# One DMA queue in the planner's order, by edges that order and do not wait

## The chip, the cores and the metric

The kernel runs on one core of one Trainium2 chip. A core has five engines with a queue of instructions each: TensorE (PE) for matmuls, VectorE (DVE), ScalarE (ACT) and GpSimd (POOL) for elementwise work, and SyncE (SP), which here issues every transfer between HBM and the core's memory. The metric is the device time of one launch in microseconds. Three runs of the kernel before took 2629.45 to 2636.64 us, median 2633.79.

## The reference

One layer of a hybrid trunk over 2048 positions of width 1024, in float32:

```python
h = rms_norm(x, norm_g)
z = h @ w_in
(aq, ak, av, af, az, bq, bk, bv, ba, bb, bz, mq, mz, gates) = _split_cols(z, IN_SIZES)
# three branches of h, each with a SiLU gate:
#   forgetting attention: 8 heads of 64, causal, score + cumsum(log_sigmoid(af + b_fg))
#   gated delta rule: 4 heads of 128, causal conv and SiLU ahead, state carried over chunks,
#     within a chunk a triangular solve with (A + I)
#   memory cross-attention: 4 heads of 128 against 256 rows of mem
# each branch @ w_branch, times sigmoid(gate + b_merge), summed; @ w_out; + x; final rms_norm
```

The comments stand for the functions of the reference. `af`, `ba`, `bb` are the few columns of logits (forget gates, decay and beta).

## The kernel before, in words

Every float32 product is made of three matmuls, of a high part and a low part of both operands. The input projection is cut into jobs. A job, `pd_in36` for instance, is one block of 128 columns of `w_in` against four groups of 512 positions, 24 matmuls each. Its weights come by `load_w`: `wr_in` (512 KB, two buffers) is loaded, ACT casts it to the high part `wh_in` (L381), POOL takes the difference as the low part `wl_in` (L385). The result of a group is emptied from PSUM into a tile `ev*`, of which there are three buffers, and stored from there (`evx` to `dv`, `evg` to `dgt`, `evl` to `dql`). Only when the store is done is the buffer free for the next group.

Beside the jobs run parts. `part_norm` makes h transposed. `part_logits` makes the logits: per group of 512 positions the matmuls `pslg`, a chain on ACT and DVE (`z`, `sg`, `e`, `l1`, up to the scan `loc` at L572), the store `dG` of the scan, and eight transposes `ptlg`. `part_gdn_inv` solves 32 x 32 blocks on DVE in two sets (`bk`, L903) and stores them as `dinv`. `part_gdn_b` reads `dinv` into `dd`, solves on from there (`pB` and later tiles), and carries the state from chunk to chunk (`chain`, with the loads `KQ`, `KV`, `Aq`, `zb`); the output of a chunk goes through `tail` (scaled, transposed in `pR`, multiplied by `zb`, stored to `dyb`). `part_fox` is the attention, with the loads `QA`, `QB`, `KA`, `KB`, `Vs`, `za`, `zl` per unit. At the end the branches are projected (`pbr`, `pba`, with the weights `wbr`, the gates `gt` and the partial sums `pp`) and the output projection `pout` follows.

What sets the order: a planner (`Plan`) keeps a clock per engine with costs of its own. Parts are generators, and each yields the time from which its next piece can run. The planner takes the pieces one after another, and so writes the program. A scheduler of the framework then gives every engine its queue out of the program: what is ready by the scheduler's own reckoning comes first, so that queue and program differ. An engine works its queue strictly in order. All transfers go through one function and so stand in SP's one queue, 1748 of them:

```python
    def move(dst, src, kb=0.0, after=0.0):
        nc.sync.dma_start(dst, src)
        return pl.dma(kb, after)
```

Its line 244 is the line of every SP row below.

Of the kernel before, what the change touches and what calls it, by code (L numbers as in the profile page):

```python
# [19 lines left out]
P = 128  # L20
EPS = 1e-6
INF = float("inf")
# [180 lines left out]
def later(*ws):  # L203
    return lambda: max(w() if callable(w) else w for w in ws)


def four(ps):
    return ps.rearrange("p (a b) -> p a b", a=4)
# [3 lines left out]
def tile_trunk(ctx, tc, x, mem, norm_g, w_in, w_v, w_lg, b_fg, b_mg, conv_w, a_log, dt_b,  # L212
               gdn_g, mem_g, w_kv, w_br, w_out, final_g, out):
    nc = tc.nc
# [7 lines left out]
    pl = Plan()  # L222
# [6 lines left out]
    def bc(ap, n):  # L229
        return ap.unsqueeze(2).to_broadcast([ap.shape[0], ap.shape[1], n])  # L230
# [12 lines left out]
# [3 lines that stand above are left out]
# [19 lines left out]
    dzb = [dram.tile([P, 4, 512], F32, name=f"dzb{g}") for g in range(NG)]  # L265
# [19 lines left out]
    def rsqrt(pool, dst, src, n, tag, after):  # L285

        yield after - AHEAD, 0.0
        s = pool.tile([P, n], F32, tag=tag + "s", name=tag + "s")
        nc.scalar.activation(s, src, AF.Sqrt)
        after = pl.op("act", 1.6, after)  # L290
        yield after - AHEAD, 0.0
        r = pool.tile([P, n], F32, tag=tag + "r", name=tag + "r")
        nc.vector.reciprocal(r, s)
        t = pool.tile([P, n], F32, tag=tag + "t", name=tag + "t")
        nc.vector.tensor_mul(t, r, r)
        nc.vector.tensor_mul(t, t, src)
        nc.vector.tensor_scalar(t, t, -0.5, 1.5, ALU.mult, ALU.add)
        nc.vector.tensor_mul(dst, r, t)
        return pl.op("dve", 0.9, after)
# [615 lines left out]
    def part_gdn_b():  # L915
# [7 lines left out]
        st = {"S": St0, "lev": 0, "chain": 0, "out": 0}  # L923

        def tmp(nm, tag, n):
            return gb.tile([P, 4, P], F32, tag=tag, name=nm, bufs=n)
# [63 lines left out]
        def chain():  # L990
            yield pl.pe + 2.0, 0.0
            for c in range(NCH):
                g, cc = divmod(c, 4)
                yield (lambda: 0.0 if st["out"] >= c - 1 else INF), 0.0
                KQ = gb.tile([P, 8, P], F32, tag="KQ", name="KQ")
                move(KQ, dkq[c], 512)
                KV = gb.tile([P, 8, P], F32, tag="KV2", name="KV2")
                move(KV, dkv[c], 512)
                Aq = tmp("Aq", "Aq", 1)
                td = move(Aq, dau[c][:, :, 1, :], 256)  # L1000
                zb = tmp("zb", "zb", 1)
                move(zb, dzb[g][:, :, cc * P:(cc + 1) * P], 256)
                St = st["S"]
                yield later(td, lambda: inv[c][1] - 1.5 if c in inv else INF, rc.when), 0.88
                E, te = inv[c]
                pZ, kb = rc.take("pZ")
                pZ = four(pZ)
                for h in range(4):
                    nc.tensor.matmul(pZ[:, h], KQ[:, h], St[:, h], start=True, stop=True)
                X = tmp("X", "ch", 3)  # L1010
                nc.vector.tensor_tensor(X, KV[:, 4:8], pZ, ALU.subtract)
                t1 = pl.dve(512, pl.pe + pl.LAT)
                rc.done(kb, t1)
                Se = tmp("Se", "ch", 3)
                nc.gpsimd.tensor_tensor(Se, St, bc(EGL[:, c, :], P), ALU.mult)
                ts = pl.pool(512, pl.pe)
                yield later(t1, te, rc.when), 0.88
                pY, kb = rc.take("pY")
                pY = four(pY)
                for h in range(4):  # L1020
                    nc.tensor.matmul(pY[:, h], E[:, h], X[:, h], start=True, stop=True)
                Y = tmp("Y", "ch", 3)
                nc.scalar.copy(Y, pY)
                t1 = pl.act(512, pl.pe + pl.LAT)
                rc.done(kb, t1)
                yield later(t1, rc.when), 0.88
                pS, kb = rc.take("pS")
                pS = four(pS)
                for h in range(4):
                    nc.tensor.matmul(pS[:, h], KV[:, h], Y[:, h], start=True, stop=True)  # L1030
                Sn = tmp("Sn", "St", 2)
                nc.vector.tensor_tensor(Sn, Se, pS, ALU.add)
                t2 = pl.dve(512, max(pl.pe + pl.LAT, ts))
                rc.done(kb, t2)
                yield later(t1, rg.when), 1.75
                pO, kb = rg.take("pO")
                pO = four(pO)
                for h in range(4):
                    nc.tensor.matmul(pO[:, h], KQ[:, 4 + h], St[:, h], start=True, stop=False)
                    nc.tensor.matmul(pO[:, h], Aq[:, h], Y[:, h], start=False, stop=True)  # L1040
                st["S"] = Sn
                st["chain"] = c + 1
                pl.add(tail(c, pO, kb, zb))

        def tail(c, pO, kb, zb):
            g, cc = divmod(c, 4)
            so = gb.tile([P, 4], F32, tag="so", name="so")
            jk = gb.tile([P, P], F32, tag="jk2", name="jk2")
            for h in range(4):
                nc.scalar.activation(jk, pO[:, h], AF.Square, accum_out=so[:, h:h + 1])  # L1050
            t1 = pl.op("act", 1.9, pl.pe + pl.LAT)
            yield t1 - AHEAD, 0.0
            nc.vector.scalar_tensor_tensor(so, so, 1.0 / P, WQ[:, c, :], ALU.mult, ALU.add)
            t1 = pl.op("dve", 0.3, t1)
            ro = gb.tile([P, 4], F32, tag="ro", name="ro")
            t1 = yield from rsqrt(gb, ro, so, 4, "gb", t1)
            ob = tmp("ob", "ob", 1)
            nc.vector.tensor_tensor(ob, pO, bc(ro, P), ALU.mult)
            t1 = pl.dve(512, t1)
            rg.done(kb, t1)  # L1060
            yield later(t1, rc.when), 0.44
            pR, kb = rc.take("pR")
            pR = four(pR)
            for h in range(4):
                nc.tensor.transpose(pR[:, h], ob[:, h], ident)
            nc.vector.scalar_tensor_tensor(zb, pR, gn_col, zb, ALU.mult, ALU.mult)
            e = pl.dve(512, pl.pe + pl.LAT)
            rc.done(kb, e)
            yield e - AHEAD, 0.0
            hi, lo = ob.bitcast(F32R), zb.bitcast(F32R)  # L1070
            nc.scalar.copy(hi, zb)
            e = pl.act(512, e)
            nc.gpsimd.tensor_sub(lo, zb, ob)
            e = pl.pool(512, e)
            yield e, 0.0
            for i, v in enumerate((ob, zb)):
                move(dyb[g][:, :, i, cc * P:(cc + 1) * P], v, 256, e)
            st["out"] = c + 1

        pl.add(chain())  # L1080
        pl.add(levels())
        yield (lambda: 0.0 if st["out"] == NCH else INF), 0.0
# [668 lines left out]
    pl.run(dense())  # L1751


def _layout(i):
    import numpy as np
    c = np.ascontiguousarray
    w = np.asarray(i["w_in"])[0]
    wd = np.concatenate([w[:, 0:1024], w[:, 1544:3592], w[:, 3600:]], axis=1)
    wl = np.concatenate([w[:, 1536:1544], w[:, 3592:3600]], axis=1)

    def chunks(m):
        k, n = m.shape
        return c(m.reshape(k // P, P, n // P, P).transpose(2, 1, 0, 3))

    wb = np.asarray(i["w_branch"])[0]
    return {
        "x": c(np.asarray(i["x"])[0]),
        "mem": c(np.asarray(i["mem"])[0]),
        "norm_g": c(np.asarray(i["norm_g"])[0]),
        "w_in": chunks(wd),  # L1770
        "w_v": c(w[:, 1024:1536].reshape(8, P, 512).transpose(1, 0, 2)),
        "w_lg": c(wl.reshape(8, P, 16).transpose(1, 0, 2)),
        "b_fg": c(np.asarray(i["b_fg"]).reshape(8, 1)),
        "b_mg": c(np.asarray(i["b_merge"]).reshape(24, P).T),
        "conv_w": c(np.asarray(i["conv_w"])[0].reshape(4, 12, P).transpose(2, 1, 0)),
        "a_log": c(np.asarray(i["a_log"]).reshape(4, 1)),
        "dt_b": c(np.asarray(i["dt_bias"]).reshape(4, 1)),
        "gdn_g": c(np.asarray(i["gdn_norm_g"]).reshape(P, 1)),
        "mem_g": c(np.asarray(i["mem_norm_g"])[0]),
        "w_kv": chunks(np.asarray(i["w_mem_kv"])[0]),  # L1780
        "w_br": c(np.stack([chunks(wb[n]) for n in range(3)])),
        "w_out": c(np.asarray(i["w_out"])[0].reshape(8, P, 1024)),
        "final_g": c(np.asarray(i["final_norm_g"])),
    }
# [17 lines left out]
```

## Time and profile before

| | |
|---|---|
| median of 3 runs | 2633.79 us |
| profiled execution | 2629.7 us, span 2627.6 us |
| PE busy | 2545.9 us, 97% |
| DVE, ACT, POOL busy | 1338.9, 1105.2, 1013.1 us |
| mean DMA rate | 149 GB/s |
| matmuls of the input projection (L401 to L403) | 3 x 1856, 0.39 to 0.40 us each |

The profiled execution is 2.1 us longer than its span, the part of a launch in which the profiled engines show nothing, and 4.1 us below the median. In a row of the profile the parts are: start in us, duration, engine, line, operation, the tile written and the tiles read, shapes, count, and in square brackets how long the engine had been idle before it and what ended that. A matmul of 512 columns shows 0.39 to 0.40 us, but the next one starts 0.23 us after it, since they are pipelined. SPq is SP's queue; an SP row is the issue of a transfer and not the transfer.

### The profile page before, as it was taken

The numbers are of one execution on the slowest core, as the hardware profiler recorded it, in microseconds if no ns is written. First come the engines' busy times: TensorE is split into PE (matmuls) and PEld (weight loads), VectorE is DVE, ScalarE is ACT, GpSimd is POOL, SyncE is SP. The second block draws the span as 40 slices with busy tenths as digits, with TensorE's granted clock in tenths as the row PEclk, the third lists the DMA queues.
The fourth block names the chain that finished last, engine by engine and source line by source line (L and its number), as shares of the span: only waits on it lengthen the run. The fifth ranks groups of instructions, "written<-read, shape, count | busy, mean of one in ns | idle before, by whom it ended". The sixth has DMA issues, their size and how long they took to land. (4 is left out here: it accounts for less than half of the span.)

```text
span 2627.6 us, 36711 instructions
## 1 busy us (share of the span) xinstructions
PE 2545.9 (97%) x12648; PEld 2112.2 (80%) x12648; DVE 1338.9 (51%) x2753; ACT 1105.2 (42%) x2287; POOL 1013.1 (39%) x818
## 2 busy tenths in 40 slices
PE   7998999999999999899999999999999999989998
PEld 6787888788888888688888888888887787877887
DVE  7452565656533337702222266666666677635433
ACT  5432234443475532134444446565556445323211
POOL 0101111221144334222232247777776768752110
PEclk9999999999999999999999999999999999999999
DMA  6223222222465564445555454344334768786432
GB/s 205 70 81 109 85 85 92 91 91 86 128 229 201 203 212 149 124 154 166 163 162 171 150 164 134 108 121 120 111 100 117 243 207 251 244 293 213 135 120 75
DMA packets 306050, 391.52 MB, mean 149 GB/s; under 512 B 62524, under 2 KB 185532, under 8 KB 305864
## 3 DMA queue, kind: packets, MB, share of 16 engines
q1 hardware_dynamic: 305864, 389.18, 46.5%
q8 instruction: 100, 1.64, 0.3%
q14 instruction: 86, 0.70, 0.1%
HBM read 238.78 MB, written 150.29 MB: 148 GB/s over the span
## 5 line engine op out<-in xcount | busy, mean ns | idle before, releaser
L401 PE MATMUL pd_in<-hh,wh_in 128*128 128x512 f32 x1856 | 746.6, 402 | 15.2 <-ACT evx L418 12.0
L403 PE MATMUL pd_in<-hh,wl_in 128*128 128x512 f32 x1856 | 728.2, 392 | 0.9
L402 PE MATMUL pd_in<-hl,wh_in 128*128 128x512 f32 x1856 | 726.0, 391 | 0.0
L385 POOL TENSOR_TENSOR wl_in<-wr_in,wh_in 128x1024 fp32r<-128x1024 f32 x84 | 202.5, 2411 | 626.0 <-ACT wh_in L381 597.8
L401 PEld LDWEIGHTS pd_in<-hh,wh_in 128*128 128x128 f32 x1856 | 350.1, 189 | 83.2 <-ACT evx L418 12.4
L403 PEld LDWEIGHTS pd_in<-hh,wl_in 128*128 128x128 f32 x1856 | 348.9, 188 | 78.6 <-POOL wl_in L385 4.0
L402 PEld LDWEIGHTS pd_in<-hl,wh_in 128*128 128x128 f32 x1856 | 350.3, 189 | 64.7
L1301 POOL TENSOR_TENSOR acc<-acc,ph 128x512 f32<-128x512 f32 (+3 forms) x288 | 318.9, 1107 | 55.7 <-ACT ph L1321 41.3
L1321 ACT ACTIVATE ph<-pst 128x512 fp32r<-128x512 f32 (+1 forms) x320 | 170.8, 534 | 159.7 <-PE pst L1315 81.2
L1278 DVE TENSOR_TENSOR plo<-pst,ph 128x512 fp32r<-128x512 f32 (+1 forms) x320 | 192.1, 607 | 83.3 <-ACT pst L1323 80.3
L1323 ACT ACTIVATE pst<-pst 128x512 f32<-128x512 f32 (+1 forms) x320 | 170.6, 533 | 0.0
L1573 POOL TENSOR_TENSOR gt<-gt,pp 128x512 f32<-128x512 f32 x64 | 86.7, 1358 | 191.6 <-DVE gt L1569 157.5
L381 ACT CAST wh_in<-wr_in 128x1024 fp32r<-128x1024 f32 x84 | 88.1, 1049 | 133.7 <-PE pd_in L402 119.2
L1188 DVE TENSOR_REDUCE nmx<-psm 128x1 f32<-128x512 f32 x192 | 128.5, 686 | 26.6 <-PE psm L1181 25.4
L1340 PE MATMUL po<-ph,Vs 128*128 128x512 f32 (+1 forms) x320 | 117.6, 368 | 1.1 <-ACT ph L1321 1.0
L474 DVE SCALAR_TENSOR_TENSOR evv<-xb,cw,evv 128x512 f32<-128x512 f32 x144 | 116.6, 810 | 3.7
L1314 PE MATMUL pst<-QA,KA 128*128 128x512 f32 (+1 forms) x320 | 116.2, 363 | 0.6 <-DVE QA L1196 0.6
L1315 PE MATMUL pst<-QB,KB 128*128 128x512 f32 (+1 forms) x320 | 116.6, 366 | 0.0
L1341 PE MATMUL pq<-plo,Vs 128*128 128x512 f32 (+1 forms) x320 | 116.1, 366 | 0.0
L1181 PE MATMUL psm<-KA,QA 68*128 68x512 f32 (+2 forms) x320 | 110.1, 375 | 4.6 <-DVE nmx L1188 3.0
L1541 PE MATMUL pbr<-yh,wbh 128*128 128x512 f32 x256 | 103.2, 404 | 9.3 <-DVE gt L1569 6.1
L1731 PE MATMUL pout<-woh,mh 128*128 128x512 f32 x256 | 100.1, 393 | 5.5 <-ACT woh L1643 5.5
(343 smaller groups left out, 4752.6 us busy)
## 6 DMA issues: line engine op xcount, KB each, us to landing
wr_in<-in_w_in SPq DMA_DIRECT2D x84, 512.0 KB
dgt<-evg SPq DMA_DIRECT2D x96, 256.0 KB
gt<-dgt SPq DMA_DIRECT2D x96, 256.0 KB
dpt<-gt SPq DMA_DIRECT2D x64, 256.0 KB
pp<-dpt SPq DMA_DIRECT2D x64, 256.0 KB
dgq<-evv SPq DMA_DIRECT2D x48, 256.0 KB
kqv<-dgq SPq DMA_DIRECT2D x16, 768.0 KB
xt<-in_x SPq DMA_DIRECT2D x16, 512.0 KB
```

Of the source, the lines that this page charges most:

```text
L385: nc.gpsimd.tensor_sub(lo, raw, hi.bitcast(F32))
L401: nc.tensor.matmul(ps, wh[:, k, :], xh[:, k, :], start=(k == 0), stop=False)
L402: nc.tensor.matmul(ps, wh[:, k, :], xl[:, k, :], start=False, stop=False)
L403: nc.tensor.matmul(ps, wl[:, k, :], xh[:, k, :], start=False, stop=(k == kt - 1))
L474: nc.vector.scalar_tensor_tensor(t, xb[:, j:j + 512], cw[:, wi, j:j + 1], t, ALU.mult, ALU.add)
L1188: nc.vector.tensor_reduce(mx, ps[:, 0:w], AX.X, ALU.max)
L1278: nc.vector.tensor_sub(plo[:, 0:w], ps[:, 0:w], ph[:, 0:w].bitcast(F32))
L1301: nc.gpsimd.tensor_add(acc[:, c0:512], acc[:, c0:512], ph[:, 0:w].bitcast(F32))
L1315: nc.tensor.matmul(ps[:, 0:w], KB[kt][:, ks], QBn[:, c0:512], start=False, stop=True)
L1321: nc.scalar.activation(ph[:, 0:w], ps[:, 0:w], AF.Exp, scale=0.125)
L1323: nc.scalar.activation(ps[:, 0:w], ps[:, 0:w], AF.Exp, scale=0.125)
L1340: nc.tensor.matmul(po[:, c0:512], V[:, 0:128], ph[:, 0:w], start=(t0 == 0), stop=(t0 == NT - 1))
```

## The change

It has two parts. At the end, when the planner has written the whole program, a loop goes through it and ties each transfer to the one before it on the same engine, by a dependency of the class NoSync. Such an edge binds the scheduler to the order and puts no semaphore wait into the queue. And the load of `zb` moves from `chain` into `tail`, which begins with a new condition: that the tail of the chunk before is through.

```diff
@@ -998,8 +998,6 @@
                 td = move(Aq, dau[c][:, :, 1, :], 256)
-                zb = tmp("zb", "zb", 1)
-                move(zb, dzb[g][:, :, cc * P:(cc + 1) * P], 256)
                 St = st["S"]
@@ -1040,10 +1038,13 @@
-                pl.add(tail(c, pO, kb, zb))
+                pl.add(tail(c, pO, kb))
 
-        def tail(c, pO, kb, zb):
+        def tail(c, pO, kb):
             g, cc = divmod(c, 4)
+            yield (lambda: 0.0 if st["out"] == c else INF), 0.0
+            zb = tmp("zb", "zb", 1)
+            move(zb, dzb[g][:, :, cc * P:(cc + 1) * P], 256)
@@ -1751,6 +1752,15 @@
     pl.run(dense())
 
+    last = {}
+    for i in list(nc.cur_bb.bb.instructions):
+        if isinstance(i, mybir.InstDMACopy):
+            if i.engine in last:
+                tc.add_manual_dep(i, last[i.engine].name, mybir.DependencyInfo(
+                    mybir.DependencyClass.NoSync, mybir.DependencyReason.DATA), reason="order")
+            last[i.engine] = i
```

The following rows show the queues that come out of it. The numbers at the tiles' names only tell them apart.

On SP near the start, before: the weights of job in36 stand among the first loads of `x`, ahead of everything that the logits store.

```order
L244 DMA xt_487<-in_x 128x1024
L244 DMA xt_491<-in_x 128x1024
L244 DMA wr_in36_0_1052<-in_w_in 128x1024
L244 DMA xt_627<-in_x 128x1024
L244 DMA xt_631<-in_x 128x1024
L244 DMA wr_in37_0_1113<-in_w_in 128x1024
```

The same loads in the changed kernel, some 25 transfers further on; `dG0` and `dG1` are the stores of the scan of the first two groups.

```order
L244 DMA dqh3_82<-evh_979 128x512
L244 DMA dql3_86<-evl_981 128x512
L244 DMA dG0_140<-loc_953 4x512
L244 DMA wr_in36_0_1052<-in_w_in 128x1024
L244 DMA dqh3_82<-evh_1048 128x512
L244 DMA dql3_86<-evl_1050 128x512
L244 DMA dG1_141<-loc_953 4x512
L244 DMA wr_in37_0_1113<-in_w_in 128x1024
```

The two weight loads have moved behind the scan's stores.

On PE at the same place, before: job in36 follows the last group of the first two jobs (`pdf1_3`).

```order
L403 MATMUL pdf1_3_983<-hh3_272,wl_in1_344 128x512
L401 MATMUL pd_in36_0_0_1109<-hh0_269,wh_in36_0_1056 128x512
L402 MATMUL pd_in36_0_0_1109<-hl0_273,wh_in36_0_1056 128x512
L403 MATMUL pd_in36_0_0_1109<-hh0_269,wl_in36_0_1058 128x512
L401 MATMUL pd_in36_0_0_1109<-hh0_269,wh_in36_0_1056 128x512
```

In the changed kernel the eight transposes `ptlg`, which read the scan, and the matmuls `pslg` of the second group (17 in all, of which the first two are shown) come between, and then job in36.

```order
L403 MATMUL pdf1_3_983<-hh3_272,wl_in1_344 128x512
L579 MATMUL ptlg_1060<-ident_63,loc_953 128x64
L580 MATMUL ptlg_1060<-ident_63,sg_1024 128x64
L579 MATMUL ptlg_1060<-ident_63,loc_953 128x64
L580 MATMUL ptlg_1060<-ident_63,sg_1024 128x64
L579 MATMUL ptlg_1060<-ident_63,loc_953 128x64
L580 MATMUL ptlg_1060<-ident_63,sg_1024 128x64
L579 MATMUL ptlg_1060<-ident_63,loc_953 128x64
L580 MATMUL ptlg_1060<-ident_63,sg_1024 128x64
L545 MATMUL pslg_1071<-hh1_270,wlh_932 128x512
L546 MATMUL pslg_1071<-hl1_274,wlh_932 64x512
```

Before, these transposes and matmuls stood in the middle of the job's third group; the next transposes, of the second group's scan, stand behind the job's fourth group in both kernels.

On SP while the inverse blocks are solved, before: the second set's `dinv1` stands between the stores of `dv2`.

```order
L244 DMA dv2_97<-evx_8835 128x4x128
L244 DMA dv2_97<-evx_8838 128x4x128
L244 DMA dinv1_195<-bk_8745 128x1024
L244 DMA dinv1_195<-tmp_8811 128x1024
L244 DMA dv2_97<-evx_8886 128x4x128
L244 DMA dv2_97<-evx_8889 128x4x128
L244 DMA dv3_98<-evx_8931 128x4x128
```

In the changed kernel it stands behind all of them, behind the gate stores `dgt` of the next jobs and ahead of the loads `U` and `dd` of the next stage.

```order
L244 DMA dv3_98<-evx_9054 128x4x128
L244 DMA dv3_98<-evx_9057 128x4x128
L244 DMA dgt0_115<-evg_9093 128x512
L244 DMA wr_in42_0_9135<-in_w_in 128x1024
L244 DMA dgt1_116<-evg_9129 128x512
L244 DMA dgt0_115<-evg_9163 128x512
L244 DMA wr_in43_0_9204<-in_w_in 128x1024
L244 DMA dgt1_116<-evg_9197 128x512
L244 DMA dinv1_195<-bk_8745 128x1024
L244 DMA dinv1_195<-tmp_8811 128x1024
L244 DMA dgt0_115<-evg_9230 128x512
L244 DMA U_9272<-dau0_160 128x4x128
```

The first set's `dinv0` moves likewise, from ahead of `dv1` to behind seven of its eight stores.

On SP where the attention begins, before: the load of a weight block for the second halves of the jobs, `wr_in42_2`, among the last chunks of the delta rule.

```order
L244 DMA Aq_12192<-dau15_175 128x4x128
L244 DMA dgt0_115<-evg_12202 128x512
L244 DMA wr_in42_2_12581<-in_w_in 128x1024
L244 DMA dgt1_116<-evg_12259 128x512
L244 DMA dyb3_126<-ob_12251 512x1x128
```

And in the changed kernel, behind the loads of the attention's first unit.

```order
L244 DMA KB0_12491<-dkh0_87 64x512
L244 DMA KB0_12491<-dkl0_91 64x512
L244 DMA Vs0_12506<-dv0_95 128x4x128
L244 DMA wr_in42_2_12581<-in_w_in 128x1024
L244 DMA dgt3_118<-evg_12473 128x512
```

It has moved past those unit loads and past the last stores of the delta rule. Elsewhere the weight loads move in the same way, from early places to the place that the planner gave them; the queues of PE, DVE, ACT and POOL hold the same work in nearly the same order (ACT has 10 fewer loads of an activation table, 102 for 112).

## The prediction

> **What bounds the kernel now.** I read the page's busy times and its costliest groups first, then the sync engine's waits, then the sequence of instructions around every place where TensorE stands still. From the page:
>
> ```profile
> PE 2545.9 (97%) x12648; PEld 2112.2 (80%) x12648; DVE 1338.9 (51%) x2753; ACT 1105.2 (42%) x2287; POOL 1013.1 (39%) x818
> L401 PE MATMUL pd_in<-hh,wh_in 128*128 128x512 f32 x1856 | 746.6, 402 | 15.2 <-ACT evx L418 12.0
> ```
>
> TensorE (PE) is busy 97% of the 2627.6 us span, in nearly the same order before and after the change. Only its idle time, about 80 us, and the slow restarts behind it can be won, and any new idle time is lost in full. The largest single wait is in the second row: 12.0 us on ACT's `evx`. The sync engine (SP) issues every transfer, and its waits by releaser say what held its queue up:
>
> ```profile
> SPq L244 <- POOL wl_in L385: 197.3, 65, 10.9
> SPq L244 <- DVE bk L903: 48.2, 2, 29.7
> SPq L244 <- DMA dyb<-zb: 29.2, 13, 3.8
> ```
>
> Columns are total us, times, longest. The middle row is two waits of `dinv` stores for the inverse chain on VectorE (DVE), one of 29.7 us. The timeline around it, SP, GpSimd (POOL) and PE:
>
> ```profile
> 1055.12 20.31 SPq L244 DMA_DIRECT2D dv<-evx  x14
> 1105.16 0.33 SPq L244 DMA_DIRECT2D dinv<-bk  x1
> 1106.66 9.66 SPq L244 DMA_DIRECT2D dv<-evx  x8
> 1076.37 2.11 POOL L420 TENSOR_TENSOR evx<-vf,evx 128x256 fp32r<-128x256 f32 x2 [1.33 <-ACT evx L418]
> 1102.77 0.39 PE L403 MATMUL pd_in<-hh,wl_in 128*128 128x512 f32 x1
> 1115.18 0.79 PE L401 MATMUL pd_in<-hh,wh_in 128*128 128x512 f32 x1 [12.03 <-ACT evx L418]
> 1122.77 0.39 PE L401 MATMUL pd_in<-hh,wh_in 128*128 128x512 f32 x1
> ```
>
> `evx` is finished at 1078.5, but its store goes out only at 1106.66, behind `dinv`; the three buffers stay full, ACT cannot empty PSUM, PE stands from 1102.77 to 1115.18. The group of 24 matmuls that follows takes 1122.77 - 1115.18 = 7.6 us.
>
> **The change part by part.**
>
> *Start, a cost.* In the new order the load `wr_in36` stands behind `dG0`, the store of the first scan `loc`, and PE's queue has the eight `ptlg` and the whole second `pslg` ahead of job in36 (both are in the rows above). Before:
>
> ```profile
> 13.37 0.38 SPq L244 DMA_DIRECT2D wr_in<-in_w_in  x1
> 87.20 0.59 ACT L551 COPY z<-pslg 64x512 f32<-64x512 f32 x1 [4.72 <-PE pslg L549]
> 88.39 0.39 PE L401 MATMUL pd_in<-hh,wh_in 128*128 128x512 f32 x1
> 88.41 1.05 ACT L381 CAST wh_in<-wr_in 128x1024 fp32r<-128x1024 f32 x1 [0.62 <-PE pdf L402]
> 89.54 2.40 POOL L385 TENSOR_TENSOR wl_in<-wr_in,wh_in 128x1024 fp32r<-128x1024 f32 x1 [6.58 <-ACT wh_in L381]
> 93.83 0.39 PE L401 MATMUL pd_in<-hh,wh_in 128*128 128x512 f32 x1
> 94.08 0.60 ACT L443 ACTIVATE evt<-pd_in 128x512 f32<-128x512 f32 x1
> 101.73 0.26 SPq L244 DMA_DIRECT2D dG<-loc  x1
> 121.38 0.24 PE L579 MATMUL ptlg<-ident,loc 64*128 64x64 f32 x1 [3.82 <-DVE loc L572]
> 121.99 0.51 PE L545 MATMUL pslg<-hh,wlh 128*128 128x512 f32 x1
> 127.36 0.39 PE L401 MATMUL pd_in<-hh,wh_in 128*128 128x512 f32 x1
> ```
>
> A weight load, from its issue to the cast that waits for it, alone and behind two others:
>
> ```profile
> 1008.13 0.33 SPq L244 DMA_DIRECT2D wr_in<-in_w_in  x1
> 1011.75 1.05 ACT L381 CAST wh_in<-wr_in 128x1024 fp32r<-128x1024 f32 x1 [2.36 <-DMA wr_in<-in_w_in]
> 1001.74 0.33 SPq L244 DMA_DIRECT2D wr_v<-in_w_v  x1
> 1008.35 1.05 ACT L854 CAST wvh<-wr_v 128x1024 fp32r<-128x1024 f32 x1 [2.22 <-DMA wr_v<-in_w_v]
> ```
>
> So 3.6 us alone, 6.6 in a crowd. The chain from `z` at 87.20 to `dG0` took 14.5 us; the cast (1.05) and the `evt` (0.60) of the job lie inside it on ACT and will not any more, so `dG0` goes at about 101.73 - 1.65 = 100.1, the load behind it at 100.4. It lands at 104.0, cast to 105.1, low part on POOL (2.40) to 107.5. PE stops at 88.39 until the scan is there, works off `ptlg` and `pslg` until about 105.5, and can go on with the job's third matmul at 107.5. A group of 24 takes 93.83 - 88.39 = 5.44 us, the job's four 21.8, of which two matmuls (0.45) are done: end at 128.9. Then `ptlg` of the next group, 0.6 us, without waiting: its scan starts from the `pslg` that ended by 105.5 and holds one `evt` of the first group (about 113), so it is there near 120, and the 3.82 us of today go. `pslg` begins at 129.5 and its 17 matmuls last 17 x 0.227 = 3.9 us, not the 127.36 - 121.99 = 5.4 of today, which came behind an idle stretch. Job in37 starts at 133.4 instead of 127.36: **+6.0 us**. Bounds: +4.5 (scan a further 1.5 us earlier) to +11 (landing 6.6, and the chain no shorter than today's 14.5). Jobs in37 to in39 keep 2 us or more by the same steps.
>
> The Trainium skill (TensorE: Matmul & The Clock Gate, "What's actually happening") says that the array's clock halves after an idle window of about 3.4 us and comes back after as much work. The trace agrees (the 3.82 us wait is followed by 1.5 us lost, the 12.03 us one by 2.2), and by that rule the 2 us before 107.5 cool nothing; with a landing of 6.6 they become 5 and some 1.7 us more, an estimate from that page, would be added.
>
> *Inverse chain, a gain.* `dinv0` moves behind seven `dv1` stores and `dinv1` behind the gate stores of job in41, so no `dv` store waits for DVE. The wait goes, 12.41 - 0.23 = 12.2, and the slow group after it, 7.59 - 5.44 = 2.15: **-14.3 us**. What could take its place is the first triangular solve, which reads `dinv`:
>
> ```profile
> 1119.12 4.60 SPq L244 DMA_DIRECT2D dd<-dinv  x8
> 1135.28 0.32 SPq L244 DMA_DIRECT2D dgt<-evg  x1
> 1156.77 0.49 PE L948 MATMUL pB<-dd,U 128*128 128x128 f32 x3
> ```
>
> All of PE comes 14.3 earlier here: the `dgt` store that now precedes `dinv1` goes at 1121, the eight `dd` loads take 4.6 us and one more gate store stands between, so they are out by about 1132 and `pB` is due at 1142.5. Ten us are left, so nothing is charged. The `dinv1` data themselves, 1105 today, are 4 us later, still ahead of 1121.
>
> *Weight loads in the middle.* They are no longer issued as soon as their buffer is free but behind the stores that the planner wrote first. The tightest are in3 and in20, of which this is in20, with the `dql` store that now stands ahead of its load:
>
> ```profile
> 253.09 0.32 SPq L244 DMA_DIRECT2D dql<-evl  x1
> 257.01 1.05 ACT L381 CAST wh_in<-wr_in 128x1024 fp32r<-128x1024 f32 x1 [4.67 <-PE pd_in L402]
> 260.59 0.50 PE L403 MATMUL pd_in<-hh,wl_in 128*128 128x512 f32 x1
> ```
>
> Issue at 253.4 and 3.6 us give 257.0, just the cast's time; with 6.6 PE loses 3.0. The others have their whole landing hidden by the 21.8 us of a job. I take 1 us for each of the two: **+2 us** (0 to +8, if six further jobs with a little more room lose 0.3 each).
>
> *First job of the attention stage.* `wr_in42_2` moves behind the key, query and value loads of unit 0, the last of which is the first row here; the second is the matmul that needs it.
>
> ```profile
> 1541.56 0.59 SPq L244 DMA_DIRECT2D Vs<-dv  x1
> 1546.48 0.40 PE L403 MATMUL pd_in<-hh,wl_in 128*128 128x512 f32 x1
> ```
>
> Issue 1542.2, landed 1545.8, cast 1546.8, low part 1549.3: **+3 us** (0 to +6, at 6.6).
>
> *Branch start, a gain.* Today `QA`, `QB` and `zl` loads stand ahead of `wbr`; now they follow it.
>
> ```profile
> 2026.38 0.38 SPq L244 DMA_DIRECT2D dgt<-evg  x1
> 2032.14 0.83 SPq L244 DMA_DIRECT2D wbr<-in_w_br  x2
> 2036.77 0.47 PE L1541 MATMUL pbr<-yh,wbh 128*128 128x512 f32 x1 [3.25 <-ACT wbh L1494]
> ```
>
> The 5.8 us from the store to `wbr` are the time in which those loads and the store pass the DMA engines; without the loads I take 2 off: **-2 us** (0 to -3.3, the whole wait of PE).
>
> *Second branch.* Its `gt` loads move later, each to its place beside the `pp` of its pair, in a stretch where the DMA engines are 84% busy and PE already waits for `gt`:
>
> ```profile
> 2255.00:2340.00 85.00, 78.91 (x347) 64.70 (x346) 37.43 (x52) 20.99 (x41) 58.59 (x48) 0.96 0.84 285
> 2333.36 0.80 PE L1541 MATMUL pbr<-yh,wbh 128*128 128x512 f32 x1 [5.00 <-DVE gt L1569]
> ```
>
> What was ahead of need becomes just in time: **+2 us** (-5, the whole wait, if the two loads of a pair arrive together; +6, as much again as the idle time of 85 - 78.91).
>
> *The `zb` load* goes into the output tail. It no longer holds SP for the store `dyb<-zb` (29.2 us in all), but nothing on PE waited for those; what it feeds is DVE's scaling behind the transpose `pR`. 0, at worst a us per stage if that cover is gone.
>
> **Sum:** +6.0 - 14.3 + 2 + 3 - 2 + 2 = -3.3. The profiled execution took 2629.7, the median is 4.1 above it; -3 from the median gives 2631 us.
>
> **The rivals.**
>
> *Late loads everywhere (slower).* My margins use today's ready times. If a store ahead of a load slips because its own buffer waits for a transfer, PE waits at each job start. The price is per job: 0.4 us in 60 jobs is 24 us, giving 2655. It decides from 11 us on, 0.2 us a job. For it speaks the 29.7 us row, a single store that stopped everything behind it; against it the 21.8 us that a job gives its successor's load of 7.1 (3.6 + 1.05 + 2.4). The Trainium skill (DMA: Bandwidth & Descriptors, "Anatomy of one DMA") states the rule under it, that a semaphore wait is served on the issuing sequencer before dispatch.
>
> *Gain without the bill (faster).* The crowding goes and the loads are all in time: 0 for the middle and the attention stage, +4.5 at the start, -5 in the second branch: -14.3 + 4.5 - 2 - 5 = -17, giving 2617. For it: SP's 197.3 us of waiting for `wl_in` are mostly loads asked for before their buffer was free, blocking stores behind them. Against: those waits stop no PE row but the one shown.
>
> *The inverse arrives late.* If `dd` lands after 1142.5, the won 12 us come back at `pB`: half of them gives 2638, all 2645. Against it the ten us above.
>
> **How the numbers follow.** The sum with its smaller uncertainties, 2623 to 2639: 0.40. Late loads everywhere, 2640 to 2665: 0.26. Gain without the bill, 2612 to 2623: 0.25. Late inverse: 0.09. A measurement of this kernel tells about 0.3%, 7.9 us, from no change, so same is 2625.9 to 2641.7. Faster: 0.25 and 0.06 from the low end of the first; slower: most of the second and 0.05 of the last, 0.30; the rest, 0.39, same. Leaving out a tenth on each side gives 2615 to 2654.
>
> **What would show it.** After: no PE wait on `evx` at 1103; `dv` stores without a stop; a new PE wait of some 11 us near 89 released by `loc`, a second of 2 at 105 by `wl_in`, none at 117; short `wl_in` waits at in20 and at 1546; `wbr` within 3 us of `dgt`. Wrong it is if `pd_in` shows waits on `wl_in` or `wh_in` at most jobs, or if `pB` waits for `dd`.

## The result, and the profile after

The changed kernel takes 2670.43 us (median of 4 runs, 2667.15 to 2674.16), the kernel before 2634.38 (4 runs, 2629.45 to 2636.64): a ratio of 1.014, 95% interval 1.012 to 1.016. It is 36 us slower, outside the predicted range. The profiled execution is the slowest of the four, 2674.16 us with a span of 2672.5; between the two profiles lie 44.9 us, and it is these that the traces below account for. They are more than the 36 us of the medians, since the profiled execution of the kernel before is 4 us faster than its median and this one 4 us slower.

From the page after, busy times and three groups; their columns are busy us, mean ns of one, and after the second bar the idle time ahead of them and what ended most of it:

```profile
PE 2561.9 (96%) x12648; PEld 2122.9 (79%) x12648; DVE 1317.6 (49%) x2753; ACT 1097.4 (41%) x2277; POOL 1020.7 (38%) x818
L401 PE MATMUL pd_in<-hh,wh_in 128*128 128x512 f32 x1856 | 749.6, 404 | 13.0 <-DVE evl L433 4.1
L403 PE MATMUL pd_in<-hh,wl_in 128*128 128x512 f32 x1856 | 730.0, 393 | 5.2 <-POOL wl_in L385 4.6
L381 ACT CAST wh_in<-wr_in 128x1024 fp32r<-128x1024 f32 x84 | 88.0, 1048 | 100.3 <-DMA wr_in<-in_w_in 74.0
```

The 12.0 us on `evx` are gone from the first group. The last row carries the loss. The page before has for the same group:

```profile
L381 ACT CAST wh_in<-wr_in 128x1024 fp32r<-128x1024 f32 x84 | 88.1, 1049 | 133.7 <-PE pd_in L402 119.2
```

Before, the cast of a weight block waited for a buffer that TensorE had to free: the data had long been there. Now ACT stands 74.0 us waiting for the load itself, while PE waits for `wl_in` only 4.6 us in all. Nearly half of the casts (40 of 84) wait for their load, and yet the projection's matmuls hardly do: besides those 4.6 us, PE waits once for `wh_in`, 3.6 us, and for the high and low parts of `w_v` 4.9 us. The stages show where the time goes. Busy us of PE, PEld, DVE, ACT, POOL with counts, the granted clock, the DMA share and GB/s, first before, then after:

```profile
0.00:240.00 240.00, 210.41 (x1030) 171.02 (x1031) 121.13 (x230) 105.13 (x163) 25.97 (x19) 0.97 0.35 116
440.00:600.00 160.00, 158.36 (x809) 129.33 (x808) 96.71 (x214) 76.04 (x187) 34.84 (x23) 1.00 0.29 97
760.00:1060.00 300.00, 296.81 (x1373) 245.02 (x1372) 134.72 (x289) 129.71 (x347) 116.01 (x100) 1.00 0.57 195
1060.00:1140.00 80.00, 67.97 (x287) 54.89 (x286) 44.11 (x62) 18.84 (x39) 24.45 (x26) 0.91 0.47 140
```

```profile
0.00:240.00 240.00, 194.98 (x930) 158.38 (x931) 118.37 (x226) 100.42 (x156) 20.83 (x17) 0.93 0.30 102
440.00:600.00 160.00, 151.02 (x788) 122.63 (x787) 100.90 (x227) 72.95 (x197) 29.86 (x19) 0.99 0.25 84
760.00:1060.00 300.00, 284.34 (x1301) 232.94 (x1300) 102.78 (x284) 146.41 (x387) 115.71 (x102) 0.97 0.61 204
1060.00:1140.00 80.00, 80.00 (x345) 64.44 (x344) 60.38 (x86) 16.64 (x43) 30.44 (x29) 1.00 0.39 112
```

PE loses busy time in the first three stages (the memory branch's attention is the second, the first stage of the delta rule the third) and is full in the fourth, where the inverse chain stood in its way before. In us, the lag of a kernel behind the one before at the same amount of TensorE work, from the start times of the matmuls in the profiled executions; the first column is the time at which the kernel before gets there, and the other kernels are those of the experiments:

| us before | after | weights free | gb free | weights, Gb free | stores only | stores from dv | dinv only |
|---|---|---|---|---|---|---|---|
| 80 | +2.7 | +1.9 | +2.2 | +3.2 | +0.9 | +0.3 | +1.7 |
| 160 | +11.5 | +2.7 | +10.9 | +2.9 | +1.7 | +1.0 | +1.6 |
| 204 | +19.4 | +7.7 | +18.5 | +7.7 | +6.8 | +1.1 | +1.5 |
| 440 | +22.3 | +7.6 | +21.6 | +7.9 | +6.8 | +0.8 | +2.6 |
| 600 | +31.5 | +7.6 | +29.4 | +8.1 | +7.2 | +0.8 | +2.6 |
| 1000 | +39.4 | +17.8 | +38.9 | +8.0 | +7.2 | +0.8 | +2.5 |
| 1040 | +51.9 | +22.1 | +47.6 | +10.6 | +7.2 | +0.8 | +2.5 |
| 1120 | +37.5 | +7.8 | +33.2 | -3.7 | -7.1 | -13.5 | -11.8 |
| 1520 | +37.1 | +7.7 | +32.8 | -3.8 | -7.2 | -13.6 | -11.9 |
| 1560 | +44.9 | +7.2 | +40.6 | -4.3 | -7.7 | -14.0 | -12.2 |
| 2000 | +43.0 | +4.1 | +39.2 | -7.5 | -5.7 | -11.5 | -11.3 |
| 2080 | +36.4 | +0.8 | +33.4 | -11.4 | -13.0 | -19.7 | -12.0 |
| 2160 | +43.1 | +5.5 | +40.4 | -8.0 | -12.1 | -19.0 | -11.9 |
| 2400 | +44.9 | +7.6 | +43.8 | -8.6 | -17.2 | -23.9 | -8.6 |

Each column is one execution against one. How far two executions differ on their own is seen in `zb_only` below, whose median is that of the kernel before: its lag is +0.4 to +0.6 from 80 to 2000, +1.9 at 2080 and 2160, and +5.0 at 2400. So steps of some 3 us behind 2000 say little.

In the places themselves: the start, where the load of job in36 stands behind the scan's store.

```profile
90.40 0.39 PE L401 MATMUL pdf<-hh,wh_in 128*128 128x512 f32 x1
102.08 0.27 SPq L244 DMA_DIRECT2D dG<-loc  x1
102.11 0.36 PE L579 MATMUL ptlg<-ident,loc 64*128 64x64 f32 x1 [10.85 <-DVE loc L572]
102.44 0.33 SPq L244 DMA_DIRECT2D wr_in<-in_w_in  x1
106.54 1.05 ACT L381 CAST wh_in<-wr_in 128x1024 fp32r<-128x1024 f32 x1 [9.58 <-DMA wr_in<-in_w_in]
107.67 2.37 POOL L385 TENSOR_TENSOR wl_in<-wr_in,wh_in 128x1024 fp32r<-128x1024 f32 x1 [90.46 <-ACT wh_in L381]
110.09 0.50 PE L403 MATMUL pd_in<-hh,wl_in 128*128 128x512 f32 x1 [0.89 <-POOL wl_in L385]
```

This is the predicted sequence, each step 2 to 2.6 us later than worked out; PE's stop at 90.40, before anything of it has happened, is 2.0 us late already. The inverse stage:

```profile
SPq L244 <- POOL evx L420: 68.2, 31, 5.0
1067.77 39.19 SPq L244 DMA_DIRECT2D dv<-evx  x15
1178.74 3.89 SPq L244 DMA_DIRECT2D dd<-dinv  x8
1194.29 1.05 PE L948 MATMUL pB<-dd,U 128*128 128x128 f32 x8
```

The `dv` stores wait for their own `evx`, at most 5.0 us (first row: total, times, longest), and between the two halves SP stands 4.7 us for `dinv` and `bk`, where one `dinv` held it for 29.7 before; PE is busy from 1060 to 1140, and the `dd` loads are out 11.7 us before `pB`, which waits for nothing. Two of the places that the prediction didn't charge: the `w_v` loads of the value jobs, and ahead of them the `Gb` load of a chunk.

```profile
1002.97 0.45 SPq L244 DMA_DIRECT2D Gb<-dG  x1
1009.41 0.21 ACT L789 ACTIVATE EGL<-Gb 128x4 f32<-128x4 f32 x1 [3.23 <-DMA Gb<-dG]
1013.02 1.30 POOL L829 TENSOR_TENSOR kqv<-kqv,eG 128x512 f32<-128x512 f32 x1
1014.35 0.32 SPq L244 DMA_DIRECT2D dkq<-kqv  x1
1039.50 0.43 SPq L244 DMA_DIRECT2D wr_v<-in_w_v  x1
1043.95 1.04 ACT L854 CAST wvh<-wr_v 128x1024 fp32r<-128x1024 f32 x1 [12.19 <-DMA wr_v<-in_w_v]
1045.05 0.52 PE L878 MATMUL pd_v<-wvh,hh 128*128 128x512 f32 x1 [3.03 <-ACT wvh L854]
1046.79 0.59 ACT L429 CAST evh<-pd_in 128x512 fp32r<-128x512 f32 x1 [1.79 <-DMA dkl<-evl]
1053.95 0.80 PE L401 MATMUL pd_in<-hh,wh_in 128*128 128x512 f32 x1 [2.69 <-DVE evl L433]
```

The store `dkq` waits in SP's queue until POOL is through with `kqv`, and every load behind it waits too. What comes late then stops ACT: 3.23 us for `EGL`, 12.19 us for `wvh`. PE waits 3.03 us for `wvh` and 1.91 for its low part. Behind `wvh` in ACT's queue stands `evh`, which empties the PSUM of the job before; DVE makes `evl` after it, and for that PE waits 2.69 us more. These are 7.6 of the 12.5 us between 1000 and 1040 in the table; in the rest the matmuls behind the waits come 0.43 us apart and not 0.23.

### The profile page after: what moved, and what is told of

Its sections match the earlier page's. It is cut to its first block, busy times and chain, and to the rows that moved or that the text cites. A ratio compares the mean times of both kernels' runs of the same rounds, so it can differ in the third digit from the quotient of the medians.

```text
span 2672.5 us, 36427 instructions
## 1 busy us (share of the span) xinstructions
PE 2561.9 (96%) x12648; PEld 2122.9 (79%) x12648; DVE 1317.6 (49%) x2753; ACT 1097.4 (41%) x2277; POOL 1020.7 (38%) x818
## 5 line engine op out<-in xcount | busy, mean ns | idle before, releaser
L453 ACT ACTIVATE evg<-pd_in,bmg 128x512 f32<-128x512 f32 x96 | 66.0, 687 | 123.3 <-PE pd_in L403 111.3
L474 DVE SCALAR_TENSOR_TENSOR evv<-xb,cw,evv 128x512 f32<-128x512 f32 x144 | 108.2, 751 | 3.6
```

## The experiments

Each time stands against runs of the kernel before on the same chip. Where only some transfers are tied, `move` takes a flag, and the loop ties each flagged transfer to the flagged one before it; lines are then some numbers lower down.

**Which transfers bring the loss.** First the `zb` move alone, with no edges.

```diff
-    last = {}
-    for i in list(nc.cur_bb.bb.instructions):
...
```

> The zb load in the tail, without the ordering edges. Theory of the late casts (the loss is that weight loads and a few other loads come late, so that the instruction that waits for them blocks its engine's queue): nothing to do with zb, the time of before within 4 us, 2630 to 2638. Theory that the zb move itself costs (SP waits, the tail's new condition): 2642 or more.

2634.09 us against 2633.55, ratio 1.0002 (0.9992 to 1.0013): nothing, so the loss comes with the edges. The edges with `zb` left where it was weren't tried. Next the planner's order for everything but the loads of weights (`w_in`, `w_kv`, `w_v`, `w_br`, `w_out`).

```diff
-            return raw, move(raw, src, kt * 64)
+            return raw, move(raw, src, kt * 64, tie=False)
...
```

> All transfers keep the planner's order except the loads of weights (w_in, w_kv, w_v, the branch and output weights), which the scheduler may hoist as before. Late casts: the steps of the changed kernel at the start (11.5 us), in20 (2), the memory branch's attention (9), the w_v loads (12.5) and in42 (8) go, the gain at the inverse chain (-14) stays, the memory rows' 9 and the delta rule's 6 stay: 2618 to 2636. Rival, the stores' strict order holds the output buffers: at most the start comes back, 2652 or more.

2634.01 us, 0.9998 (0.9988 to 1.0008). Without the order on the weight loads the whole loss of 36 us is gone; it is no gain yet, since the lag of 14.5 us from 600 to 1040 takes back what `dinv` brings. Its page:

```profile
L384 ACT CAST wh_in<-wr_in 128x1024 fp32r<-128x1024 f32 x84 | 88.2, 1050 | 136.1 <-PE pd_in L405 125.4
```

The cast waits for its load no more; for `Gb`, which is still tied, ACT's `EGL` waits 49.5 us in this run (9.8 in the kernel before). Then the opposite: all as before, except that the `dv` stores, the load of `bk` and the `dinv` stores are tied among themselves.

```diff
-                move(dinv[s][:, 0], E.rearrange("p j i -> p (j i)"), 512)
+                move(dinv[s][:, 0], E.rearrange("p j i -> p (j i)"), 512, tie=True)
...
```

> The kernel before, with edges only among the stores of dv, the load of bk and the stores of dinv; zb as before. Both theories: the 12 us wait on evx and its slow restart go and nothing else moves: 2617 to 2623, the wait at 1103 absent. If the gain needs the whole queue in order, 2630 or more.

2618.51 us, 0.9939 (0.9922 to 0.9956). The table shows the step between 1040 and 1120: -14.3.

**What else is late.** The weights and also `kqv` and `Gb` free:

```diff
-                nxt[c] = kqv, Gb, move(Gb, dG[g][:, cc * P:(cc + 1) * P].partition_broadcast(P), 256) + 1.0
+                nxt[c] = kqv, Gb, move(Gb, dG[g][:, cc * P:(cc + 1) * P].partition_broadcast(P), 256, tie=False) + 1.0
...
```

> As the one with free weights, and the loads of kqv and Gb (delta rule, first stage) free too. Late loads in general: the 6 us lost there come back besides, so 4 to 9 us less than with free weights alone, about 2612 to 2630. If only weights matter: the same as with free weights within 2 us.

2620.45 us, 0.995 (0.9935 to 0.9965): from 720 to 1040 the lag grows by 2.5 us and no longer by the 14 of the run before. With the loads of `x` and of the memory rows free as well:

```diff
-        return xt, move(xt, src[row: row + P, :], 512)
+        return xt, move(xt, src[row: row + P, :], 512, tie=False)
...
```

> The planner's order for all transfers except the loads of weights, kqv and Gb, and now also the loads of x and mem tiles and of the memory norm's scale. Late loads: the 2 to 3 us lost before 80 us and the 5 lost at the memory rows (near 204) come back too: 2609 to 2617. If these were lost to something else: 2619 to 2622, as with weights and Gb free.

2623.19 us against 2632.04, 0.9965 (0.995 to 0.998), a miss: the lag at 204 us is +6.0 and was +7.7. So the loss at the memory rows isn't their loads' place in the order alone. And `kqv` and `Gb` alone free, with the weights tied:

> The planner's order for all transfers but kqv and Gb; the weight loads stay late. The runs so far give the loads of the weights 2669 - 2634 = 35 us and, with those free, kqv and Gb another 13.5. If the two costs add (theory: each is a stop of ACT at its own place), the time is 2669 - 13.5, about 2656 (2651 to 2661), and the lead at 1000 us is some 8 us below that of the changed kernel while the 9 us at 440 to 560 and the 9 us at 180 to 206 stay. Rival: they hide one another (a load that waits anyway makes the other free), and 2664 to 2670 comes out, or they add up to more because a late Gb also makes weight loads late, below 2651.

2670.53 us against 2631.04, 1.0144 (1.0127 to 1.0161). The costs don't add. Between 600 and 1040 the lag grows by 20.4 us with both late, 18.2 with only the weights late, 14.5 with only `kqv` and `Gb` late, 2.5 with neither: the two late loads cost mostly the same time, and taking one away leaves the other. The rival that they hide one another holds, the time half a us above its 2664 to 2670.

**Stores alone.** The planner's order for the stores; every load free.

```diff
-            outs.ask(e, lambda: move(dh[g][:, i, :], th.bitcast(F32), 256))
+            outs.ask(e, lambda: move(dh[g][:, i, :], th.bitcast(F32), 256, tie=True))
...
```

> Edges among the stores alone, in the planner's order; every load is free. Late loads: nothing is lost any more, and the 14 us at the inverse chain are won: 2609 to 2618. Rival, the strict order of the stores holds output buffers and costs by itself: 2625 or more.

2616.17 us against 2632.04, 0.9936 (0.9918 to 0.9954): the gain at `dinv`, a further one at the branches, and a loss of 5.1 us between 160 and 204. To place that one, the same from the first `dv` store on only:

```diff
-        if tie:
+        if tie and n >= begin[0]:
...
```

> Stores alone in the planner's order as in stores_only, but only from the first dv store (about 1055 us) on; before it nothing is tied. It tells what the 7 us of lost time at 204 us of stores_only come from. Theory: from the edges between the stores of the start (dqh, dql, dG, dF), so that here the lead at 204 to 1040 us is that of dinv_only, +1.5 to +2.7, and the time is 2616 - 5 = 2611 (2607 to 2615). Rival: the loss at 204 comes from the order of the engines' queues that the scheduler makes anyway, or is won back later in stores_only; then 2614 to 2619.

2608.76 us against 2631.04, 0.9918 (0.9898 to 0.9937), the lowest ratio of all. It overlaps with that of `stores_only`, so that the 5 us rest on the lag: it is +1.1 at 204 and was +6.8, and what differs up to there is the order of the early stores. The wait of 12.0 us on `evx` is gone from the first group of its page:

```profile
L406 PE MATMUL pd_in<-hh,wh_in 128*128 128x512 f32 x1856 | 745.5, 402 | 3.2 <-DVE evt L449 3.0
```

**How a late load costs time where PE doesn't wait for it.** The memory branch's attention loses 9.2 us between 440 and 600. In the changed kernel at its second late block, job in35:

```profile
504.23 0.42 SPq L244 DMA_DIRECT2D wr_in<-in_w_in  x1
508.81 1.05 ACT L381 CAST wh_in<-wr_in 128x1024 fp32r<-128x1024 f32 x1 [1.33 <-DMA wr_in<-in_w_in]
509.93 2.39 POOL L385 TENSOR_TENSOR wl_in<-wr_in,wh_in 128x1024 fp32r<-128x1024 f32 x1 [8.14 <-ACT wh_in L381]
509.96 2.45 DVE L687 TENSOR_SCALAR mst<-mst 128x2 f32<-128x2 f32 x2
512.46 0.47 ACT L691 ACTIVATE pr<-psc,mst 128x256 f32<-128x256 f32 x1 [2.60 <-DVE mst L687]
514.21 0.63 PE L709 MATMUL ptm<-ident,pr 128*128 128x128 f32 x4 [2.25 <-DVE pr L697]
```

Two things meet the softmax: the cast stands in ACT's queue ahead of `pr`, and the subtraction, which follows the cast at once, runs on POOL just as DVE has its small step `mst` to do. PE waits 2.25 us for the softmax and not for a weight. In one run the cast and with it the subtraction of the three blocks in question were put 12 us later into the program:

```diff
+    LATE = ("in34_0", "in35_0", "in18_0")
-            return raw, move(raw, src, kt * 64)
+            return raw, move(raw, src, kt * 64) + (12.0 if nm in LATE else 0.0)
...
+            if nm in LATE:
+                tc.add_manual_dep(new, q[-2].name, ...)
```

> The changed kernel, in which only the casts of three weight blocks (in34, in35, in18) are placed 12 us later in ScalarE's queue, by the planner's time and an edge; their loads stand where they stood but for what follows from that. Theory that a late weight load hurts where its cast blocks ScalarE's queue: the 9 us lost between 440 and 570 fall to 0 to 3, in all 2660 to 2665, and the waits of the transposes ptm for the softmax there fall below 1 us. Rival, the weights or the DMA traffic reach TensorE late by themselves: no change, 2668 to 2673, or worse.

2667.02 us against 2632.04, 1.0132 (1.011 to 1.0153), 2 us above the expected range; the stretch loses 2.0 us, as expected, and no `ptm` waits longer than 0.5. To part the two, the subtraction alone later, the cast where it was:

```diff
+            if nm in LATE:
+                pl.at(t, lambda: cast(raw))
+                t += 12.0
...
```

> The changed kernel, in which for the three jobs in34, in35 and in18 only the subtraction on POOL (wl_in) is put 12 us later into the program and tied behind POOL's instruction before it, as in casts_later; the cast (wh_in) stays where the changed kernel has it in ACT's queue, ahead of the softmax's pr. It tells which of two stops the memory attention. Theory ACT: the late cast stops ACT and the pr behind it; then the stretch from 440 to 600 us loses what the changed kernel loses there, +7 to +9 us. Theory POOL: the subtraction, which follows the cast at once, falls on the softmax's small steps on DVE (mst, 2.38 us beside wl_in in the changed kernel, 0.16 without), and DVE waits for it; then the stretch loses +2 to +4, as casts_later does with +2.0, since the casts alone still cost some 0.8 us. Total 2664 to 2672 in both.

2670.46 us against 2633.79, 1.0139 (1.0121 to 1.0157), and the stretch loses 5.1 us, between the two expectations. At the same place:

```profile
500.26 1.05 ACT L389 CAST wh_in<-wr_in 128x1024 fp32r<-128x1024 f32 x1 [1.36 <-DMA wr_in<-in_w_in]
501.38 0.29 DVE L705 TENSOR_SCALAR mst<-mst 128x2 f32<-128x2 f32 x2
502.91 0.62 DVE L715 TENSOR_SCALAR pr<-pr,mst 128x256 f32<-128x256 f32 x2
503.41 0.63 PE L727 MATMUL ptm<-ident,pr 128*128 128x128 f32 x4
```

The cast still waits for its load, 1.36 us (1.33 in the changed kernel), and stands ahead of `pr`, but PE waits for nothing here. Across this block, from 484 to 488 us of the kernel before, the lag stays at 18.9, where in the changed kernel it grows from 27.4 to 29.7; at the other two blocks it doesn't grow either. The 5.1 us come in three steps of 1.5 to 1.7 further on, each where the moved subtraction now falls:

```profile
512.89 2.38 POOL L398 TENSOR_TENSOR wl_in<-wr_in,wh_in 128x1024 fp32r<-128x1024 f32 x1
514.32 1.37 DVE L715 TENSOR_SCALAR pr<-pr,mst 128x256 f32<-128x256 f32 x2
515.48 0.70 PE L727 MATMUL ptm<-ident,pr 128*128 128x128 f32 x4 [1.23 <-DVE pr L715]
```

The two `pr` of the next head take 1.37 us beside it and not 0.62, and PE waits 1.23. So it is the subtraction that costs, beside `mst` or beside `pr`, wherever it falls on a step of the softmax on DVE; the late cast ahead of `pr` costs nothing that the lag shows. With both moved, 2.0 us stay, in three steps of 0.7 to 0.9 whose cause is open. The times of these runs say nothing between them: 3 us are within their scatter, and the reading rests on one profiled execution of each.

Last, every cast tied behind the instruction that the program has ahead of it on ACT, so that no cast stands earlier in ACT's queue than the planner put it:

```diff
+                tc.add_manual_dep(new, q[-2].name, mybir.DependencyInfo(
+                    mybir.DependencyClass.NoSync, mybir.DependencyReason.DATA), reason="cast")
...
```

> The changed kernel, in which every cast of an input weight block keeps its place in the program behind the ScalarE instruction ahead of it, so that the scheduler cannot hoist it. Theory of the blocked queue: a part of the loss comes back, where the planner's place is later than the scheduler's, 2650 to 2666. Rival: unchanged, 2668 to 2673.

2684.75 us against 2632.04, 1.0196 (1.0176 to 1.0217), a miss. The memory attention no longer loses (43.2 to 43.9 us of lag from 440 to 600), but from 240 to 400 the lag grows from 24.3 to 43.3, and now it is the projection that waits; its PE waits:

```profile
PE pd_in L408 <- POOL wl_in L390: 12.8, 11, 1.3
PE pd_in L406 <- ACT wh_in L381: 10.6, 9, 3.0
```

With loads this late, the planner's place for all casts is no better: what the memory attention wins is lost where PE waits for the casts themselves.

## Why the prediction was wrong

**The step that failed** is the sentence "The others have their whole landing hidden by the 21.8 us of a job", with the bill of +2 us (0 to +8) under *Weight loads in the middle*. With the weight loads alone taken out of the order, the kernel is 36 us faster (2634.01 us for 2670.43). The margin was taken from the time at which PE needs the low part. But before PE a load meets ACT and POOL, whose queues the scheduler orders by its own reckoning: ACT waits 74.0 us for the loads, and the subtraction on POOL, the emptying of PSUM and the softmax of other parts shift with it or fall on one another. For in3 and in20, where PE is the one that waits, the term held: the lag grew by 0.8 at in3 and by 1.4 at in20, 2.2 for the +2 charged. The stretches for which nothing was charged hold 38.6 of the 48.2 us between the sum's -3.3 and the 44.9 of the profiles: the memory rows +9 (5 of them by the stores), the memory attention +9.2, the first stage of the delta rule from 600 to 1000 +7.9, the `w_v` loads +12.5. In the last two the late `kqv` and `Gb` alone would have cost most of it too. For the memory attention the way from late load to lost time is shown by runs; for the stretches from 600 to 1040 the runs show which loads cost, and the way is read from the waits.

The rival *Late loads everywhere* gave 2655 by a price per job start. Its direction was right and its mechanism half: stores that wait in SP's queue do hold the loads up, as with `dkq` at 1014, but PE waits for `wl_in` 4.6 us in all. The sign at which the prediction told the reader to look, `pd_in` waiting at most jobs, isn't there; the waits of ACT would have shown it.

By the other steps:

- *Start*, +6.0 (4.5 to 11): +11.5 at 160, of which 2.7 are there at 80, ahead of the place (1.7 in `dinv_only` too, where nothing is tied so early), and 8.8 fall here. The chain was right in kind, and its errors cancel: from `z` to `dG0` it took 12.2 us and not 12.85, the load 4.1 us from issue to cast and not 3.6, and behind the 10.85 us gap the matmuls of `pslg` came 0.43 us apart until 106.7 and only then 0.23, which the sum didn't charge. Its comparison was misread: in the kernel before, job in37 had begun at 114.67, and twelve of its matmuls stand ahead of the transposes at 121.38, so that 127.36 is its thirteenth. These 12 x 0.227 = 2.7 us are missing from the +6.0; with them the sum gives 8.7.

```profile
114.67 0.39 PE L401 MATMUL pd_in<-hh,wh_in 128*128 128x512 f32 x1
```

- *Memory rows* (the 256 rows of `mem`, loaded, normalised and transposed around 200 us), not charged: 9 us from 160 to 210. 5 are due to the stores' order (`stores_only` against `stores_from_dv`). Some 2 more are the scaling of the second load of the memory rows: on DVE it fell beside `wl_in` and took 3.43 us where it takes 1.28 elsewhere. What the other 2 us are stays open.

```profile
212.13 0.33 SPq L244 DMA_DIRECT2D xt<-in_mem  x1
220.50 3.43 DVE L352 SCALAR_TENSOR_TENSOR xt<-xt,rs,mg_bc 128x1024 f32<-128x1024 f32 x1
220.51 2.34 POOL L385 TENSOR_TENSOR wl_in<-wr_in,wh_in 128x1024 fp32r<-128x1024 f32 x1 [26.65 <-ACT wh_in L381]
223.99 1.97 PE L360 MATMUL ptx<-ident,xt 128*128 128x128 f32 x8 [11.93 <-DVE xt L352]
```

- *Inverse chain*, -14.3: -14.4 between 1040 and 1120 in the changed kernel, -14.3 in `dinv_only`. The late inverse didn't come.
- *First job of the attention stage*, +3 (0 to +6): +7.8. The step was right, and so was the issue: 1542.2 and the lag of 37.1 make 1579.3, and the load left at 1579.67. The landing was mis-sized: the cast came 6.1 us after the issue, behind the unit loads, and PE waited twice, 4.9 us, with slow matmuls behind, which the bound had left out.

```profile
1579.67 0.50 SPq L244 DMA_DIRECT2D wr_in<-in_w_in  x1
1585.74 1.04 ACT L381 CAST wh_in<-wr_in 128x1024 fp32r<-128x1024 f32 x1 [1.98 <-DMA wr_in<-in_w_in]
1586.84 0.50 PE L401 MATMUL pd_in<-hh,wh_in 128*128 128x512 f32 x1 [3.61 <-ACT wh_in L381]
1589.29 0.79 PE L403 MATMUL pd_in<-hh,wl_in 128*128 128x512 f32 x1 [1.25 <-POOL wl_in L385]
```

- *Branch start*, -2 (0 to -3.3): -6.6 from 2000 to 2080. `wbr` follows `dgt` by 2.1 us (2066.87 and 2068.93), and no `pbr` waits more than 0.27 us there; the slow matmuls behind the old wait (0.43 us apart from 2039) go too, which the bound had left out. But it is given back by 2160 (+6.7): PE waits 2.21 us for ACT's `pst` at 2136, and the rest isn't explained.
- *Second branch*, +2: from 2160 to 2400 +1.8, by luck. The step went the other way: the wait of 5.00 us for `gt` goes (the lag falls from 41.3 at 2320 to 35.0 at 2340), and a wait of 5.9 us for the weights `wbh` at 2387, which nobody had charged, takes it back. That wait is there with the weight loads free too (6.5), so it isn't their order; its cause is open. `dinv_only` and `zb_only`, which tie nothing there, grow by 3.3 and 3.1 in this stretch.
- *`zb`*, 0: 0, by `zb_only`.

## What to carry to other kernels

An order over a queue is worth having among the transfers that block one another, here the stores from `dv` on (-22 us), and costs where it takes a load from its early place. The margin of a load isn't told by the time at which the bounding engine needs it: ask which queue takes it first, what stands behind it there, and beside what the work made of it will then run. Edges on one queue leave the other queues as the scheduler made them, for the old ready times; that this mismatch is behind the loss is argued and not shown, and tying the casts as well made the time longer.

## What the runs showed of the hardware

An instruction on DVE that begins beside a long one on POOL can be held until that is through: the first `mst` (128 x 2) above took 2.4 of the row's 2.45 us, where two take 0.29 in the run without `wl_in` beside them, two `pr` took 1.37 us for 0.62, and `xt` took 3.43 us for 1.28, each beside a `wl_in` of 2.3 to 2.4 us. The Trainium skill (SBUF — State Buffer, "Who interferes with whom") says that a DVE instruction in a two-port mode contends with GpSimd for a shared pair of ports, and that the one that issues first holds the pair for its whole length while the other is blocked; the trace agrees for `mst`, issued at 509.96 and ending at 512.4 beside a `wl_in` from 509.93 to 512.3. What wasn't expected is its weight: the memory attention loses or keeps most of its 9.2 us by where `wl_in` falls, with POOL busy for 29.9 of its 160 us and DVE for 100.9.
